# Expert weights as whole matrices, a dense gather of two units, and the last modulation vector beside the router

## The chip, the cores and the metric

The kernel runs on one core of a Trainium2 chip. The core has TensorE (PE in the rows; the loading of its stationary operand has a row of its own, PEld), VectorE (DVE), ScalarE (ACT), GpSimd (POOL) and SyncE (SP), which here only issues transfers. Every load from HBM goes through one queue, in the order in which SP issues it, and 16 DMA engines move the bytes. The metric is the device time of one execution in microseconds; lower is better. The profile is of one execution on the chip; its span runs from the first instruction to the last.

## The reference, cut to what matters

Two blocks follow each other on x (256 tokens by 1024). The first has attention, a gated delta rule and a mixture of experts; its output is normalised and goes into the second, a transformer block whose shifts, scales and gates (`mod`, six vectors of 1024) come from a conditioning vector, and whose attention also looks at 256 context tokens. Cut:

```python
# first block, at its end
h = rmsnorm(x, ffn_norm)
g_sel = argmax(h @ w_group)                   # one of 4 groups
within = top2(softmax((h @ w_router)[g_sel])) # two of its 8 experts, weights normalised
for e in all 32 experts:
    y += ((silu(h @ w_gate[e]) * (h @ w_up[e])) * combine[:, e]) @ w_down[e]   # 1024x256, 1024x256, 256x1024
x = rmsnorm(x + y, final_norm)
# second block
mod   = split(silu(c) @ w_mod + b_mod, 6)     # w_mod is 1024x6144
mod_c = the same with c_ctx
hc = rmsnorm(ctx) * (1 + scale_c) + shift_c   # keys and values of the context: hc @ w_in
x = x + g1 * attention(rmsnorm(x) * (1 + scale) + shift, hc)
x = x + g2 * swiglu(rmsnorm(x) * (1 + scale2) + shift2)
```

## The kernel before

The program has stages: "a" (first attention and delta rule, with its weights split into a high and a low part so that three float32r products stand for one float32 product), "c" (router and experts) and "d" (second block). A scheduler orders the instructions of each engine when the program is built; where `PE.start()` and `PE.stop()` enclose code, the order on TensorE is that in which the code is written.

All large weights come in blocks of 1 MiB (128 partitions by 2048 float32), `load_block`, line 157. Each takes a buffer: one of a ring of nine, or, in the expert stage, one of the further pools named in `SLOTS` ("r" ring, "x" three, "y" seven, "z" two, which is 21 with the ring). A block is issued when its buffer is free, and SP issues in a fixed order, so one block that waits holds up all behind it.

The experts run in eight units of four. Each unit has room for 32 tokens of each of its experts. Per unit:

- `gather(u)` (line 1051) picks the tokens with a one-hot matrix S: 16 matmuls in float32 of x against S, in two halves, each evicted with the gain `gF` into `xg`.
- gate and up (`pgu`): for each of 8 slices k and each of the 4 experts j one matmul in a quarter of the array's columns. `wexp` (line 1027) cuts the four gate matrices by k: block q holds the slices 2q and 2q+1 of all four experts, so its rows in HBM are four pieces of 2 KB a partition.
- the hidden values are turned (`pth`), then `pyd`, the down products in two halves nh of 512 columns; a block of `w_down` is one (nh, k2) of four experts.
- each half is split into yh and yl and added into four PSUM banks `acc` through a one-hot matrix ST.

At unit 4 (`IFU`) the order changes: only ring and "x" buffers stay, plus two of a new pool "w". The context is loaded, normalised through diagonal matrices (`ctx_norm`), and four of its five projections (`ctx_heads`, with the columns of w_in in `KVU`) run between the products of units 5 and 6, where the scheduler puts them. `kv_a` and `qk_heads` each hold a head norm (ACT square, DVE sum, GpSimd power, DVE product) and then transposes on TensorE. A branch, `overflow()`, stands ahead of unit 4 for experts with over 32 tokens.

The modulation vectors: `mod_steps` yields once per block of `w_mod`, 24 in all, 8 matmuls each. `more_mod` takes such steps as filler inside stage "a", by the numbers in `MODR` (in the triangular solves) and `MODS` (behind the projections). At the router a loop takes whatever is left.

In the profile, a float32 matmul shows as two records on TensorE, and a float32r matmul as one.

Of the kernel before, what the change touches and what calls it, by code (L numbers as in the profile page):

```python
# [9 lines left out]
F32 = mybir.dt.float32  # L10
# [7 lines left out]
P = 128  # L18
# [87 lines left out]
def tile_kernel(ctx: ExitStack, tc: tile.TileContext, I, out, dbg=None):  # L106
# [9 lines left out]
    def open_stage(name, psum, base=False):  # L116
# [9 lines left out]
        S_["junk"] = {"a": ("zg", 2), "c": ("jk", 1), "d": ("prb2", NPR)}[name]  # L126
# [30 lines left out]
    def load_block(src, name, extra=None):  # L157

        if extra:
            t = extra[0].tile([P, 2048], F32, tag="rx", name=name, bufs=extra[1])  # L160
# [219 lines left out]
    def mod_steps():  # L380


        for n in range(6):
            p = psm([P, 256], "pmod", "mo")
# [11 lines left out]
            part = tmp_([P, 8, 32], "part", "part")  # L396
            DVE.transpose(part, p.rearrange("p (c k) -> p k c", k=8))
            DVE.tensor_tensor(mod[:, n], part[:, :, 0::16], bc(bmc[:, n], 2), op=ALU.add)
            if n in (1, 4):
                DVE.scalar_tensor_tensor(mod[:, n], mod[:, n], 1.0, bc((gN1, gN2)[n // 4], 2), op0=ALU.add, op1=ALU.mult)  # L400
            yield
# [373 lines left out]
    def out_steps():  # L775
        for kb in (2, 3, 0, 1):
            hi, lo = w_blk[kb]
            for kk in range(2):
                k = 2 * kb + kk
                for tt in range(2):  # L780
                    ts = slice(tt * P, (tt + 1) * P)
                    for nh in range(2):
                        ns = slice(nh * 512, nh * 512 + 512)
                        mm3(po2[2 * tt + nh], mixh[:, k, ts], mixl[:, k, ts], hi[:, kk, ns], lo[:, kk, ns], k == 4, k == 3)
                        yield
# [85 lines left out]
    rx3p = rx2.enter_context(tc.tile_pool(name="rx3", bufs=1, side="right", reuse_waits="tile"))  # L871
# [18 lines left out]
    for tt in range(2):  # L890
        jk = tmp_([P, D], "jk", "jk", bufs=2, dt=BF16)
        if tt == 0:
            i = ACT.activation(jk, x[:, 0], AF.Square, accum_out=ssq[:, 0:1])
# [7 lines left out]
    S_["mod"] = None  # L901
    for _ in mods:
        if S_["mod"]:
            after(S_["mod"], pl_ins)
# [55 lines left out]
    PE.matmul(prk[:, 1], lhsT=trisb, rhs=sel[:, 1], start=False, stop=True)  # L960
    rrp = at([P, 2, 32], "rrp", "rrp")
# [9 lines left out]
    def one_hots(g):  # L971
        S[g] = at([P, 2, 8, 32], "S", "S")
        for ts in (slice(0, 1), slice(1, 2)) if g == 0 else (slice(0, 2),):
            DVE.tensor_tensor(S[g][:, ts], io[:, None, None, :].to_broadcast([P, ts.stop - ts.start, 8, 32]),
# [3 lines left out]
    one_hots(0)  # L978
    pov = psm([1, 1], "pov")
# [29 lines left out]
    DVE.tensor_tensor(ovc, ovm, comb, op=ALU.mult)  # L1009
# [4 lines left out]
    DVE.tensor_copy(combr[:, :, :, 4:6], r1[:, :, None, None].to_broadcast([P, 2, 8, 2]))  # L1014

# [4 lines left out]
    pools = {"r": None, "x": (S_["base"], RX), "y": (rx2p, RX2), "z": (rx3p, RX3)}  # L1020
# [6 lines left out]
    def wexp(w, u, part, name):  # L1027
# [25 lines left out]
    def gather(u):  # L1053

        if u % 2 == 0 and u:
            one_hots(u // 2)
        xg = c2.tile([P, 8, P], F32, tag="xg", name=f"xg{u}", bufs=2)
        for kp in range(2):
            p = pt_([P, 4, P], "y", "pgat")
            for kk in range(4):  # L1060
                for tt in range(2):
                    PE.matmul(p[:, kk], lhsT=x[:, tt, 4 * kp + kk::8], rhs=S[u // 2][:, tt, u % 2 * P:u % 2 * P + P],
# [782 lines left out]
```

## Time and profile before

| | us |
|---|---|
| three timed runs, median (lowest to highest) | 851.44 (848.9 to 851.9) |
| the profiled execution, its own time | 851.4 |
| span of that execution | 849.6 |

| engine | busy us | share of the span | instructions |
|---|---|---|---|
| TensorE (matmul) | 784.6 | 92% | 6412 |
| TensorE (weight load) | 647.7 | 76% | 6412 |
| VectorE | 424.1 | 50% | 937 |
| ScalarE | 296.1 | 35% | 526 |
| GpSimd | 107.4 | 13% | 93 |

200.18 MB are moved, 236 GB/s over the span. A share is a mean over stages with different limits, so it says little by itself: the transfers are near their limit for half of the time and almost idle for the other half. What a part of the change is worth is read from its stage: which wait ends last there. A buffer that comes free late shows as a wait of the transfer queue for an engine, and only later as a wait of an engine for data. The granted clock of TensorE has two levels, 2.4 GHz (1.00 in the windows) and 1.2 GHz (0.50); a stretch between is a mixture.

### The profile page before, as it was taken

Reading aid. Unit: us, or ns where it says so; the run is one execution under the profiler, and the core shown is the slowest. Engines: PE = TensorE matmul, PEld = TensorE weight load, DVE = VectorE, ACT = ScalarE, POOL = GpSimd, SP = SyncE. Lnnn points to the kernel's source line nnn. Section 1 sums busy time; section 2 is a strip of 40 time slices with the busy share of each in tenths; the row PEclk is TensorE's granted clock in tenths of the full one; section 3 lists DMA queues with packets and bytes.
Section 4 is the critical chain, followed back from the end, with each engine's and each line's share of the span. In section 5 each row is a group of like instructions: output and inputs, shape, how many; then the busy total and the mean of one; then the engine's idle time right before and its main releaser. Section 6 shows DMA issues by size and latency. Waiting matters only on the chain.

```text
span 849.6 us, 15290 instructions
## 1 busy us (share of the span) xinstructions
PE 784.6 (92%) x6412; PEld 647.7 (76%) x6412; DVE 424.1 (50%) x937; ACT 296.1 (35%) x526; POOL 107.4 (13%) x93
## 2 busy tenths in 40 slices
PE   7999999999789989896998899799996999999997
PEld 6887887967656646673865799688875999999996
DVE  4766553565422111223132769887656555455545
ACT  5432233453110000101011765287723444434431
POOL 5001000142000000000000376400021200000000
PEclk9999999999889998987999999899999999999999
DMA  7999778488799999999599506111431756555201
GB/s 212 350 385 380 278 284 305 171 308 302 279 388 386 386 386 387 378 386 370 198 390 377 169 5 161 59 51 50 150 105 47 257 188 197 179 174 193 100 2 49
DMA packets 123415, 200.18 MB, mean 236 GB/s; under 512 B 15480, under 2 KB 62000, under 8 KB 123344
## 3 DMA queue, kind: packets, MB, share of 16 engines
q1 hardware_dynamic: 123152, 199.08, 67.3%
q8 instruction: 51, 0.84, 0.4%
q0 software_dynamic: 192, 0.11, 0.1%
q14 instruction: 20, 0.16, 0.1%
HBM read 198.23 MB, written 1.05 MB: 235 GB/s over the span
## 4 chain that ended last, share of the span: by engine, by line
PE 46%; DVE 7%; POOL 3%; ACT 2%; issue 2%; POOLq 0%; DVEq 0%; ACTq 0%
PE pfu L99 7%; PE pfg L99 7%; PE pf L99 7%; PE sc L99 3%; PE pgat L99 3%; PE pgu L99 2%; PE po L99 2%; PE ptp L102 2%; PE pyd L99 2%; PE ckbp L99 2%; PE pqa L99 1%; PE pqb L99 1%; POOL latl L192 1%; PE acc L99 1%; PE pt L99 1%
## 5 line engine op out<-in xcount | busy, mean ns | idle before, releaser
L99 PEld LDWEIGHTS pgat<-S,x 128*128 128x128 f32 x256 | 62.4, 335 | 2.8 <-DVE xg L1066 1.1
L99 PE MATMUL pgat<-S,x 128*128 128x128 f32 x256 | 63.0, 405 | 0.6 <-PEq L1215 0.5
L99 PE MATMUL pfu<-hif,fuh 128*128 128x256 f32 x176 | 50.3, 286 | 1.6 <-ACT fuh L185 1.6
L99 PE MATMUL pfu<-hif,ful 128*128 128x256 f32 x176 | 50.5, 287 | 0.9 <-POOL ful L192 0.8
L99 PE MATMUL pfu<-lof,fuh 128*128 128x256 f32 x176 | 50.2, 285 | 0.0
L99 PE MATMUL pfg<-hif,fgl 128*128 128x256 f32 x160 | 45.5, 284 | 0.0
L99 PE MATMUL pfg<-lof,fgh 128*128 128x256 f32 x160 | 45.5, 284 | 0.0
L99 PE MATMUL pfg<-hif,fgh 128*128 128x256 f32 x160 | 45.5, 284 | 0.0
L1066 DVE TENSOR_TENSOR xg<-pgat,cols__83 128x512 f32<-128x512 f32 x15 | 10.4, 692 | 63.8 <-PE pgat L99 63.8
L192 DVE TENSOR_TENSOR fdl<-fd,fdh 128x512 fp32r<-128x512 f32 x44 | 27.5, 688 | 28.8 <-ACT fdh L185 28.8
L99 PE MATMUL pyd<-ed,hid 128*32 128x512 f32 x256 | 34.1, 665 | 3.8 <-ACT hid L1341 3.8
L1335 ACT ACTIVATE sg<-pgu,r1s 128x256 f32<-128x256 f32 x8 | 3.8, 474 | 96.6 <-PE pgu L99 73.9
L99 PEld LDWEIGHTS pfu<-hif,fuh 128*128 128x128 f32 x176 | 34.3, 195 | 1.8 <-ACT fuh L185 1.8
L99 PEld LDWEIGHTS pfu<-hif,ful 128*128 128x128 f32 x176 | 34.3, 195 | 1.3 <-POOL ful L192 1.3
L99 PE MATMUL pf<-fdl,fh 128*128 128x512 f32 x88 | 35.1, 399 | 0.0
L185 ACT ACTIVATE fuh<-fu 128x1024 fp32r<-128x1024 f32 x22 | 22.1, 1053 | 37.0 <-issue 28.6
L185 ACT ACTIVATE fdh<-fd 128x1024 fp32r<-128x1024 f32 x22 | 22.1, 1053 | 36.8 <-issue 35.8
L99 PE MATMUL pf<-fdh,fh 128*128 128x512 f32 x88 | 34.7, 394 | 0.0
L99 PEld LDWEIGHTS pfu<-lof,fuh 128*128 128x128 f32 x176 | 34.2, 194 | 0.0
L99 PE MATMUL pf<-fdh,fl 128*128 128x512 f32 x88 | 34.0, 392 | 0.0
L192 DVE TENSOR_TENSOR fgl<-fg,fgh 128x512 fp32r<-128x512 f32 x40 | 27.7, 755 | 9.3 <-ACT fgh L185 9.3
L99 PEld LDWEIGHTS pfg<-hif,fgh 128*128 128x128 f32 x160 | 30.9, 193 | 0.4
(704 smaller groups left out, 2156.6 us busy)
## 6 DMA issues: line engine op xcount, KB each, us to landing
eg<-in_w_gate_dram SPq DMA_DIRECT2D x32, 1024.0 KB, 14.0
eu<-in_w_up_dram SPq DMA_DIRECT2D x32, 1024.0 KB, 13.9
ed<-in_w_down_dram SPq DMA_DIRECT2D x32, 1024.0 KB, 13.4
wmod<-in_w_mod_dram SPq DMA_DIRECT2D x24, 1024.0 KB, 10.3
fg<-in_w_gate_dram SPq DMA_DIRECT2D x11, 1024.0 KB, 5.6
fu<-in_w_up_dram SPq DMA_DIRECT2D x11, 1024.0 KB, 5.7
fd<-in_w_down_dram SPq DMA_DIRECT2D x11, 1024.0 KB, 5.1
kv<-in_w_in_dram SPq DMA_DIRECT2D x5, 1024.0 KB, 13.5
```

The lines of the kernel that those rows point to most:

```text
L99: return self._keep(self.engine.matmul(*args, **kwargs))
L102: return self._keep(self.engine.transpose(*args, **kwargs))
L185: S_["hi"] = ACT.activation(hf[:, s], vf[:, s], AF.Copy)
L192: i = (POOL if c in pool else DVE).tensor_tensor(lf[:, s], vf[:, s], hf[:, s], op=ALU.subtract)
L1066: DVE.tensor_tensor(xg[:, ks], p, bc(gF[:, ks], P), op=ALU.mult)
L1335: ACT.activation(sg, pgu[:, 0], AF.Silu, scale=r1s[:, u:u + 1])
```

## The change

1. An expert's gate, up or down matrix is one block: 128 partitions by one piece of 8 KB. Block j now belongs to expert j, so each pass needs all four blocks from its start, and frees them at its end.
2. x is split into xhi and xlo (float32r, laid out by slices k). `gather(g)` serves two units: 32 float32r matmuls of 256 columns, four evictions. Unit 2 adds xhi and xlo into `acc` by an identity, so the adds of x behind unit 7 go, and x's own memory becomes a buffer ("p").
3. The buffers are ring nine, x three, y seven, p one: 20. "z" is gone, and "w" has one in place of two.
4. From unit 4 to the end of unit 7 TensorE's order is as written. Projections of the context stand between gate and up, and, with the turning of the hidden values between their halves, ahead of down. Both down halves stand ahead of the splits and of acc. The context's rows are scaled ahead of plain transposes. Columns 1792 are used in unit 5, given up and loaded again for the second block.
5. Twenty blocks of w_mod are left in stage "a"; the last vector's four come behind the blocks of w_out, three are multiplied behind the logits and the fourth behind the ranks. Its PSUM bank is that of acc2.
6. The last block of the first output projection runs by halves of the tokens.

```diff
 def wexp(w, u, part, name):
...
-        src = w[u // 2, 4 * (u % 2):4 * (u % 2) + 4]
-        if name == "ed":
-            src = src.rearrange("e (p k) c -> p e k c", k=2)[:, :, part % 2, part // 2 * 512:part // 2 * 512 + 512]
-        else:
-            src = src.rearrange("e (p k) c -> p e (k c)", k=8)[:, :, part * 512:part * 512 + 512]
+        src = w[u // 2, 4 * (u % 2) + part].rearrange("(p k) c -> p k c", p=P)
...
+    xhi, xlo = (at([P, 2, 8, P], nm, nm, dt=F32R) for nm in ("xhi", "xlo"))
+    identr = at([P, P], "identr", "identr", dt=F32R)
+    for tt in range(2):
+        xk = x[:, tt].rearrange("t (p k) -> t k p", k=8)
+        after(ACT.activation(xhi[:, tt], xk, AF.Copy), jk_ins)
+
+    PE.start()
+    for i in range(3):
+        next(mods)
...
+    pmod5 = next(mods)
...
     one_hots(0)
+    xk = x.rearrange("t a (p k) -> t a k p", k=8)
+    for i in range(4):
+        ks = slice(2 * i, 2 * i + 2)
+        S_["xlo"] = DVE.tensor_tensor(xlo[:, :, ks], xk[:, :, ks], xhi[:, :, ks], op=ALU.subtract)
+        after(S_["xlo"], S_["S"])
...
-    pools = {"r": None, "x": (S_["base"], RX), "y": (rx2p, RX2), "z": (rx3p, RX3)}
+    pools = {"r": None, "x": (S_["base"], RX), "y": (rx2p, RX2), "p": (pers, 1, "x")}
...
+    def gather(g, tags=("y", "y")):
+
+        if g:
+            one_hots(g)
+        xg = [c2.tile([P, 4, 256], F32, tag="xg", name=f"xg{g}", bufs=2) for _ in range(2)]
+        for kp in range(4):
+            p = pt_([P, 2, 256], tags[kp % 2], "pgat")
+            for kk in range(2):
+                parts = [(tt, xp) for xp in (xhi, xlo) for tt in range(2)]
+                for n, (tt, xp) in enumerate(parts):
+                    PE.matmul(p[:, kk], lhsT=xp[:, tt, 2 * kp + kk], rhs=S[g][:, tt], start=n == 0, stop=n == 3)
...
+    CTX = {4: (None, None), 5: ((1792, lambda b=None: ctx_v(0, b)), (512, ctx_ka)),
+           6: ((1280, lambda b=None: ctx_kb(0, b)), (1536, lambda b=None: ctx_kb(1, b))), 7: (None, None)}
...
             if half == 0:
                 gate_ins = last
+                if u == 4:
+                    hcT = ctx_norm()
+                elif u > 4 and CTX[u][0]:
+                    CTX[u][0][1]()
...
+        if u >= IFU and CTX[u][1]:
+            CTX[u][1][1](turn_hid)
+        else:
+            turn_hid()
...
-MODR = [2, 2, 2, 2, 2, 2]
-MODS = [0, 1, 2, 0, 1, 0, 1, 0, 2, 2, 2, 2, 2, 1, 0, 0, 0, 0]
+MODR = [2, 2, 2, 1, 1, 1]
+MODS = [0, 1, 1, 0, 1, 0, 1, 0, 1, 2, 1, 2, 1, 0, 0, 0, 0, 0]
...
-SLOTS = "r" * 4 + "ry" * 4 + "yyyr" + "xz" * 2 + "x"
+SLOTS = "r" * 4 + "ry" * 4 + "yyyr" + "xxxp"
...
-KVU = ((512, 1280), (1536, 1792), (), (2048,))
```

What this moves on the engines, at three places. First the transfer queue of SP behind the last block of w_out (`wo`), up to the first expert blocks (`eg`, `eu`, `ed` are gate, up and down). Before:

```order
L164 DMA wo_2328<-in_w_out_dram 128x2x1024
L164 DMA eg<-in_w_gate_dram 128x4x512 x4
L164 DMA eu<-in_w_up_dram 128x4x512 x3
L164 DMA ed<-in_w_down_dram 128x4x512 x2
L164 DMA eg<-in_w_gate_dram 128x4x512
L164 DMA eu<-in_w_up_dram 128x4x512
L164 DMA eg<-in_w_gate_dram 128x4x512 x2
```

After, the same place:

```order
L164 DMA wo_2284<-in_w_out_dram 128x2x1024
L164 DMA wmod<-in_w_mod_dram 128x2x1024 x4
L164 DMA eg<-in_w_gate_dram 128x2048
L164 DMA eu<-in_w_up_dram 128x2048 x2
L164 DMA ed<-in_w_down_dram 128x2048 x2
L164 DMA eg<-in_w_gate_dram 128x2048 x6
L164 DMA eu<-in_w_up_dram 128x2048 x5
```

Four blocks of w_mod now stand ahead of the experts, and an expert block has one run of 2048 where it had four of 512.

Second, TensorE from the logits (`pl`) over the ranks (`prk`) to the first gate products. Before:

```order
L99 MATMUL pl<-wr,hT 128x36 x16
L99 LDWEIGHTS trisb
L99 MATMUL prk<-sel,trisb 128x32
...
L99 MATMUL pov<-ones_96,ovn 1x1
L99 MATMUL pgat<-S,x 128x128 x16
L99 MATMUL pgu<-eg,xg_2635 32x256 x32
```

After:

```order
L99 MATMUL pl<-wr,hT 128x36 x16
L99 MATMUL pmod<-wmod,sil 32x256 x24
L99 LDWEIGHTS trisb
L99 MATMUL prk<-sel,trisb 128x32
...
L99 MATMUL pmod<-wmod,sil 32x256 x8
L99 MATMUL pov<-ones_96,ovn 1x1
L99 MATMUL pgat<-S,xhi 128x256 x2
L99 MATMUL pgat<-S,xlo 128x256 x2
```

The products of the last modulation vector stand on both sides of the ranks, and the gather takes two columns of S's halves at once, from xhi and then from xlo.

Third, TensorE in the seventh unit, from its gate products to its down products (`ckbp` is a projection of the context, `pqk` the transposes behind its head norm). Before:

```order
L99 MATMUL pgu<-eg,xg_3885 32x256 x32
L99 MATMUL pgu<-eu,xg_3885 32x256 x15
L102 MATMUL pqk<-cst,qn__3935 128x128 x4
L99 MATMUL cvbp<-kv_3958,hcT 128x256 x16
L99 MATMUL pgu<-eu,xg_3885 32x256 x17
L99 LDWEIGHTS esel
L99 MATMUL pst<-rrT,esel 128x256
L102 MATMUL pth<-cst,sg 128x128 x2
L99 MATMUL pyd<-ed,hid 32x512 x16
```

After:

```order
L99 MATMUL ckbp<-kv_3953,hcT 128x256 x16
L102 MATMUL pqk<-cst,qn__4023 128x128 x4
L99 MATMUL pgu<-eu,xg_3893 32x256 x16
L99 MATMUL pgu<-eu,xg_3894 32x256 x16
L99 LDWEIGHTS esel
L99 MATMUL pst<-rrT,esel 128x256
L99 MATMUL ckbp<-kv_3963,hcT 128x256 x8
L102 MATMUL pth<-cst,sg 128x128 x2
L99 MATMUL ckbp<-kv_3963,hcT 128x256 x8
L102 MATMUL pqk<-cst,qn__4105 128x128 x4
L99 MATMUL pyd<-ed,hid 32x512 x16
```

Both transposes behind a head norm now stand directly behind the projection that feeds the norm, and ahead of up and of down.

## Rows read from the trace of the kernel before

**Rows 1.** The page, 40 slices of 21.24 us: what the transfers moved

```profile
GB/s 212 350 385 380 278 284 305 171 308 302 279 388 386 386 386 387 378 386 370 198 390 377 169 5 161 59 51 50 150 105 47 257 188 197 179 174 193 100 2 49
```

**Rows 2.** Windows: length, busy us of five engines (instructions), granted clock, DMA share, GB/s

```profile
6.00:10.00 4.00, 2.58 (x21) 2.21 (x20) 1.98 (x8) 1.59 (x3) 2.14 (x4) 1.00 1.07 355
...
50.00:100.00 50.00, 49.17 (x523) 41.17 (x522) 30.50 (x87) 15.85 (x33) 5.94 (x5) 1.00 0.95 349
...
82.00:88.00 6.00, 5.89 (x54) 5.86 (x51) 2.58 (x8) 1.02 (x2) 2.03 (x4) 1.00 1.02 410
...
228.00:232.00 4.00, 4.00 (x74) 2.42 (x77) 0.69 (x1) 0.00 (x0) 0.00 (x0) 1.00 0.33 71
...
240.00:246.00 6.00, 5.53 (x33) 1.23 (x32) 0.69 (x1) 0.98 (x2) 0.00 (x0) 0.59 1.04 385
...
270.00:290.00 20.00, 18.41 (x187) 13.72 (x189) 3.32 (x9) 0.86 (x2) 0.00 (x0) 1.00 1.05 387
...
414.00:424.00 10.00, 10.00 (x88) 8.20 (x90) 1.55 (x3) 0.60 (x1) 1.30 (x1) 1.00 0.09 19
```

**Rows 3.** Waits of TensorE, 50 to 200 us: total, times, longest us

```profile
PE pkq L99 <- DVE kn L594: 0.7, 1, 0.7
...
PE po L99 <- ACT mixh L758: 0.2, 1, 0.2
```

**Rows 4.** Groups of TensorE, 228 to 470 us: busy us, mean ns, idle before

```profile
L99 PE MATMUL pgat<-S,x 128*128 128x128 f32 x226 | 55.8, 402 | 0.5 <-PEq L1215 0.5
```

**Rows 5.** Timeline of SP's issues: start us, length us, transfer, count

```profile
2.62 1.53 SPq L164 DMA_DIRECT2D w<-in_w_in_dram  x2
...
70.94 25.07 SPq L164 DMA_DIRECT2D wmod<-in_w_mod_dram  x6
...
402.78 20.58 SPq L164 DMA_DIRECT2D ed<-in_w_down_dram  x4
...
441.23 12.92 SPq L164 DMA_DIRECT2D ed<-in_w_down_dram  x4
```

**Rows 6.** Waits of the transfer queue, 400 to 430 us: total, times, longest us

```profile
SPq L164 <- PE pgu L99: 18.8, 5, 17.2
```

**Rows 7.** Timeline of TensorE: start us, length us, output, count, idle before and releaser

```profile
142.30 1.93 PE L99 MATMUL pmod<-wmod,sil 128*32 128x256 f32 x30
...
228.27 3.66 PE L99 MATMUL pgu<-eg,xg 128*32 128x256 f32 x64
...
240.65 5.72 PE L99 MATMUL pyd<-ed,hid 128*32 128x512 f32 x32 [0.47 <-ACT hid L1341]
...
288.62 3.64 PE L99 MATMUL pyd<-ed,hid 128*32 128x512 f32 x32 [0.47 <-ACT hid L1341]
...
293.44 3.85 PE L99 MATMUL pgat<-S,x 128*128 128x128 f32 x16
...
383.03 4.05 PE L99 MATMUL ckbp<-kv,hcT 128*128 128x256 f32 x18
...
391.23 0.69 PE L102 MATMUL pqk<-cst,qn__3725 128*128 128x128 f32 x4 [3.15 <-DVE qn__3725 L1104]
394.97 0.39 PE L99 MATMUL pst<-rrT,esel 32*128 32x256 bf16 x1 [3.05 <-DVE kLb L1166]
...
465.02 1.92 PE L99 MATMUL pyd<-ed,hid 128*32 128x512 f32 x16
468.13 0.73 PE L99 MATMUL acc<-yh,ST 128*128 128x512 f32 x2 [1.19 <-ACT yh L1352]
```

**Rows 8.** Timeline of VectorE, columns as in rows 7

```profile
219.95 0.76 DVE L974 TENSOR_TENSOR S<-cst,rrp 128x256 f32<-128x256 f32 x2
...
469.39 1.28 DVE L1359 TENSOR_TENSOR x<-x,acc 128x512 f32<-128x512 f32 x2 [0.59 <-PE acc L99]
```

**Rows 9.** The chain that ended last: start us, length us, what

```profile
735.97 5.75 PE pfg L99 x48
```

**Rows 10.** The page's groups: busy us, mean ns, idle before

```profile
L1335 ACT ACTIVATE sg<-pgu,r1s 128x256 f32<-128x256 f32 x8 | 3.8, 474 | 96.6 <-PE pgu L99 73.9
```

More of the change, by code (lines that the diff above doesn't have):

```diff
@@ L159, in load_block @@
         if extra:
-            t = extra[0].tile([P, 2048], F32, tag="rx", name=name, bufs=extra[1])
+            t = extra[0].tile([P, 2048], F32, tag=extra[2] if len(extra) > 2 else "rx", name=name, bufs=extra[1])
         else:
@@ L395, in mod_steps, with mod_end @@
                     yield
[L396 to L401, printed above, removed]
+            if n < 5:
+                mod_end(n, p)
+                yield
+        yield p
+    def mod_end(n, p):
+        part = tmp_([P, 8, 32], "part", "part")
+        S_["part"] = DVE.transpose(part, p.rearrange("p (c k) -> p k c", k=8))
+        DVE.tensor_tensor(mod[:, n], part[:, :, 0::16], bc(bmc[:, n], 2), op=ALU.add)
+        if n in (1, 4):
+            DVE.scalar_tensor_tensor(mod[:, n], mod[:, n], 1.0, bc((gN1, gN2)[n // 4], 2), op0=ALU.add, op1=ALU.mult)
     MODA = MODS[:14]
@@ L1199, in proj_ctx, with ctx_v, ctx_ka, ctx_kb @@
                 S_["cx"].append(m)
-        return p
-    def ctx_heads():
-        kv_a(proj_ctx(512, "cka"), 1, "tr")
-        yield
-        for half in range(2):
-            qk_heads(proj_ctx(1280 + 256 * half, "ckb"), half, 3, "tr", s=1)
-            yield
-        for half in range(2):
-            S_["vb"] = (ACT.copy if half else DVE.tensor_copy)(vb[1][:, :, half * 256:half * 256 + 256], proj_ctx(1792 + 256 * half, "cvb"))
-            yield
+            if tt == 0 and between:
+                between()
+        return p
+    def ctx_v(half, between=None):
+        p = proj_ctx(1792 + 256 * half, "cvb", between)
+        S_["vb"] = (ACT.copy if half else DVE.tensor_copy)(vb[1][:, :, half * 256:half * 256 + 256], p)
+    def ctx_ka(between=None):
+        kv_a(proj_ctx(512, "cka", between), 1, "tr")
+    def ctx_kb(half, between=None):
+        qk_heads(proj_ctx(1280 + 256 * half, "ckb", between), half, 3, "tr", s=1)
     def overflow():
@@ L1219, in overflow @@
                 for tt in range(2):
-                    PE.matmul(p[:, tt * P:(tt + 1) * P], lhsT=x[:, tt, k::8], rhs=ident, start=True, stop=True)
+                    for xp in (xhi, xlo):
+                        PE.matmul(p[:, tt * P:(tt + 1) * P], lhsT=xp[:, tt, k], rhs=identr, start=xp is xhi, stop=xp is xlo)
                 DVE.tensor_scalar(hT[:, k], p, gF[:, k:k + 1], None, op0=ALU.mult)
@@ L1272, in tile_kernel @@
             c2 = S_["tmp"]
-        if u not in xgs:
-            xgs[u] = gather(u)
+        if u // 2 not in xgs:
+            xgs[u // 2] = gather(u // 2, ("y", "y" if u < IFU else "cx"))
         if u and u % 2 == 0:
@@ L1295, in tile_kernel @@
                 DVE.tensor_copy(gcol[:, i:i + 1], pgc[:, 0:1])
-            ring_slot()
-            cx = load_block(I["ctx_2"][0].rearrange("(a p) d -> p a d", p=P), "cx")
+            PE.start()
         if u == 5:
-            hcT = ctx_norm()
             queue.append("r")
-        if u >= 5:
-            for c0 in KVU[u - 5]:
-                ring_slot()
+        first.setdefault(u, [])
+        for i, (w, nm) in enumerate(((wg_, "eg"), (wu_, "eu"), (wd_, "ed"))):
+            if len(first[u]) == i:
+                first[u].append([wexp(w, u, q, nm) for q in range(4)])
+            if u >= IFU and i < 2 and CTX[u][i]:
+                c0 = CTX[u][i][0]
+                if c0 != 1792:
+                    ring_slot()
                 kvw[c0] = load_block(cols(w_in2, c0), f"kv{c0}")
-                next(ctxh)
-        if u not in first:
-            loads(u)
         if u == 7:
@@ L1328, in tile_kernel @@
             acc = [psm([P, 512], "acc0"), psm([P, 512], "acc1", "mo")] + [accp_.tile([P, 512], F32, tag=f"acc{i}", name=f"acc{i}") for i in (2, 3)]
+        if u == 2:
+            for tt in range(2):
+                for nh in range(2):
+                    for xp in (xhi, xlo):
+                        PE.matmul(acc[2 * tt + nh], lhsT=identr, rhs=xp[:, tt, :, 64 * nh:64 * nh + 64].rearrange("t k p -> t p k"),
+                                  start=False, stop=False)
         p = pt_([P, 256], "tr", "pst")
```

125 lines of the change are left out of this document (60 added, 65 removed).

## The prediction

> **What bounds the kernel now.** I read four views, in this order. The 40 slices of the page [rows 1] first: from about 230 us to 460 us the transfers run at 386 to 390 GB/s with one hole, and after 480 us they never matter again. So only the first 480 us can react to how the experts are loaded; the last 370 us are the second block, which the change leaves alone apart from how x is stored. The windows [rows 2] give the stream's speed and its holes: 387 GB/s in 270 to 290 us, 19 GB/s in 414 to 424 us (10 us lost) while TensorE is busy all 10 us, and 71 GB/s in 228 to 232 us, where all 21 buffers are full and unit 0 has not yet freed one. What the transfer queue waited for in 400 to 430 us is TensorE: 17.2 us in one wait [rows 6], and the four down loads of unit 6 take 20.58 us to issue [rows 5]. So the stage has two limits by turns: the stream from 232 to about 345 us, and TensorE in the units that also carry the context's projections. TensorE's largest group there is the gather, 55.8 us for 226 records [rows 4]. Ahead of 205 us TensorE is the limit: 49.17 of 50 us busy [rows 2], and from 50 to 200 us it waits 3.4 us in six waits of 0.7 to 0.2 us, none of them for a transfer [rows 3].
>
> **The change part by part.** All sums stand against the profiled execution: span 849.6 us, 851.4 us with the 1.8 us around it, which is the median of the runs shown (851.44 us).
>
> *Whole matrices.* The same 96 MiB are loaded, but one row of a partition is now 8 KB in one piece and not four pieces of 2 KB. What size of piece does to the speed is in the windows [rows 2]: pieces of 1 KB (w_in, 6 to 10 us) move at 355 GB/s, of 2 KB (experts, 270 to 290 us) at 387, of 4 KB (w_mod, 82 to 88 us) at 410; what was on its way then is in the queue's rows [rows 5]. One block of 1 MiB then takes 2.95, 2.71 and 2.56 us. 8 KB is not in the trace. Each halving of the number of pieces saved less, 0.24 and then 0.15 us, so the next saves some 0.08: 2.48 us. The other end is 2.56 us, if a piece of 8 KB does no better than 4 KB, and 2.71 if nothing is gained. I take 2.52, midway of the first two, since those lie on the curve. At the point where the stream starts again after the router 76 of 96 blocks are still to come (20 buffers full), so 76 x (2.71 - 2.52) = 14.4 us less, between 0 and 17.5.
>
> *The gather.* Before, each unit had 16 matmuls of float32 with 128 columns in two halves of about 3.85 us, as at 293.44 us [rows 7], 7.7 us a unit, 62 us in all. Now two units share 32 float32r matmuls of 256 columns. Matmuls of that shape run one per 0.12 us in the feed-forward part (48 in 5.75 us [rows 9]), so 3.8 us for two units, 15 us in all: 46 us of TensorE less. The stream is slower than this work, so by itself it gives nothing; it gives back the hole at 414 to 424 us, 10 us. In units 0 to 3 TensorE then needs 3.7 + 3.6 + 3.6 + 2.9 + 1.9 us and some 2 us of small products, about 18, against 12 x 2.52 = 30 us of stream. In unit 6 it needs gather 3.8, gate 3.7, projection 7.2, the wait of a head norm, up 3.6, projection 7.2, another wait, down 3.6, acc 2.9. The wait is from the end of the projection at 387.08 to the transposes at 391.23 us [rows 7], 4.15 us, and the fixed order puts nothing of TensorE into it. Sum 40.3 us, against 36.1 us of stream (12 expert blocks, two of w_in). Unit 5 with one such wait needs 33 against 36. So TensorE ends unit 6 some 4 us later than its data, frees its down buffers that late, and unit 7's stream waits some 2 us for them: +2, between 0 and +6. Net of the hole: -8.
>
> *First unit.* DVE must now write the four xlo parts (512 columns, 0.64 us each by the adds of that shape [rows 8]) after S, which is ready at 220.7 us [rows 8]; ACT's xhi lies beside the logits. Gather, its eviction on ACT (eight of 0.47 us [rows 10]) and the gate overlap by parts, so the gate ends near 227.5 us and not 231.9 [rows 7]: 4 us earlier. But there are 20 buffers and not 21, and four of them hold w_mod until its products behind the logits free them at about 217 us; the queue then has eight blocks to bring from 209.7 us, to about 230 us. At 231.5 us, where the stream began again before with 21 blocks in, 20.6 are in: 0.4 blocks, +1.0 us, between -1 and +3. The hole at 228 us is gone, and the 21st buffer that hid it too, so it gives nothing more.
>
> *The last modulation vector.* Its four blocks cost TensorE 30 records in 1.93 us [rows 7], 64 records in 4.1 us, in a stretch where TensorE is the limit. They go to where it waits for DVE's choice of experts. Three of the four blocks were filler inside the triangular solves, where less filler can turn into a wait, so I take 2.5 of the 4.1 us: -2.5, between 0 and -4.1. Everything behind moves with it. The DVE part (one transpose, one add) comes behind the routing weights, where DVE has nothing else that the gather needs; without that cover it would stand ahead of the first eviction, at well under the 0.64 us of a full tile [rows 8].
>
> *The end of the stage.* Before, the last down load is issued by 454.15 us [rows 5], and its products come in two halves with the acc products between, the second at 465.02 us, the last acc product done near 469.6 us [rows 7]. In whole matrices all 32 products need the block of the fourth expert: 3.6 us after the last landing and not 1.9. At the lower clock level (0.59 granted in 240 to 246 us [rows 2]) the same 32 took 5.72 us [rows 7], and TensorE will have waited for data. So +2, between +0.5 and +4. The adds into x (two of 0.64 us [rows 8]) are gone from the path since x is summed in PSUM; eight products of x stand in unit 2 instead, where there is slack: -0.7, between 0 and -1.3.
>
> *At nothing:* context rows scaled ahead and not by a diagonal (off the path while TensorE has slack; it shortens unit 4 by some 6 us of slack), kv 1792 loaded a second time behind the stage, where the stream is idle [rows 1], the order of the last out-projection block (x adds begin 1.4 us earlier, TensorE runs straight on there).
>
> Sum: -14.4 - 10 + 2 + 1.0 - 2.5 + 2 - 0.7 = -22.6. Span 827.0, with 1.8 around it **828.8 us**. With all ends at their best 818, at their worst 854; all at one end is unlikely, so 818 to 837 is the forecast's own range.
>
> **Rivals.**
>
> *Pieces of 8 KB are no faster.* Then the first part does not do what it says: 387 GB/s stay, 14.4 us are lost, 843.2 us. Against it: 355, 387, 410 GB/s rise with the piece [rows 2]. For it: nothing here shows a piece over 4 KB, and the load of one matrix may be limited elsewhere. The Trainium skill, DMA: Bandwidth & Descriptors, section "Where 436 GB/s comes from", says that loads from HBM are bound at about 358 GB/s per core. By that the stream could not gain and this rival would be the result; the rows at 387 and 410 GB/s already stand above it, so I give it little weight.
>
> *The fixed order waits.* In units 5 and 6 TensorE stands at three head norms in a row. If each costs more than 4.15 us (at 394.97 us the trace has another wait of 3 us for the same PSUM bank's copies) and the projection behind it starts at the lower clock level, its 7.2 us growing to up to 14, TensorE ends unit 6 some 14 us behind its data and not 4. Unit 7's buffers come 10 us later: 838.8 us. For it: the stall that made the hole at 414 us began behind the first of these norms. Against it: in the new order the transposes of the hidden values stand between the halves of the projection, so that DVE and ACT work beside it.
>
> *TensorE goes slow (the slower side).* With 18 us of work in 30 us it now waits for each set of four matrices, and none of a set can start until the fourth is there. In units 4 to 7 it has 4 x 14 + 7.7 + 4 x 7.2 + 2 = 94.5 us of work in 135 us of stream. At half clock each of these costs another; 40 us are covered by waiting, and after that each comes out at the end. The 22.6 us are eaten when 63 of the 94.5 run at the lower level; with all of them 883 us. For it: 0.59 in 240 to 246 us, 5.72 us and not 3.64 for the same products [rows 2, 7]. Against it: in 270 to 290 us, with waits for the hidden values in it, the clock is 1.00, and a TensorE that falls behind no longer waits. The Trainium skill, TensorE: Matmul & The Clock Gate, section "Loop structure matters more than you think", warns of just this loop, a wait for a transfer between groups of matmuls; the 240 us row agrees, and by it this rival would be likelier than I make it.
>
> **How the numbers follow.** Forecast 828.8 us with chance 0.64; fixed order 838.8 with 0.15; no faster pieces 843.2 with 0.12; TensorE slow, 855 to 883, with 0.05; something not seen 0.04, half of it slower. The range 816 to 841 holds the forecast, the fixed order's case and the lower edge of the third. About 0.5% (4.3 us) is what a measurement of this kernel can tell from no change. Faster by more: 0.89; within: 0.04; slower: 0.07.
>
> **What would show each step.** Windows of the expert stage at 410 to 423 GB/s, not 387, show the first term; a window without a hole around units 5 to 7, and a transfer queue that waits little for TensorE, show the second. The gather's group should read 128 records, and 15 us, not 62. The first out-projection and the router should come 2 to 3 us earlier, the first gate near 225 us, the last acc product near 447 us, and from there to the end some 380 us as before. A granted clock under 0.8 over most of units 4 to 7, or down products that stand behind the head norms with the queue idle, would make it wrong; so would a first unit whose down blocks land after 240 us.

## The result: 11.7 us less, where 22.6 were forecast

| | before | after | ratio (95% interval) |
|---|---|---|---|
| timed runs, median (lowest to highest) | 850.97 us (848.9 to 851.9) | 839.32 us (836.76 to 841.26) | 0.9865 (0.9826 to 0.9904) |
| the same two kernels, measured again | 852.27 us (849.43 to 853.69) | 837.18 us (832.93 to 839.01) | 0.984 (0.9818 to 0.9861) |

The change is faster, by 11.7 us, and by 15.1 in the second measurement (differences of the medians). The forecast was 828.8 us, 22.6 less, with a range of 816 to 841 that holds the result near its upper end. The profiled execution of after took 841.26 us (span 839.5). It is read here against the one of before (851.4 us, span 849.6).

What the transfers moved, in the page of after (40 slices of 20.99 us):

```profile
GB/s 219 343 389 346 213 251 331 102 313 294 396 369 419 420 418 417 387 409 407 414 308 297 135 20 178 30 52 51 152 146 33 272 171 182 201 175 178 100 2 50
```

The 386 of [rows 1] have become 420, but one larger dip is left: 308 in the slice from 420 us. Windows of after, columns as in [rows 2]:

```profile
219.00:222.00 3.00, 2.65 (x23) 1.86 (x14) 3.00 (x7) 0.20 (x1) 0.00 (x0) 0.65 1.00 407
222.00:225.00 3.00, 3.00 (x19) 2.17 (x18) 2.93 (x13) 1.54 (x4) 0.00 (x0) 0.50 1.01 418
...
231.00:234.00 3.00, 3.00 (x64) 1.80 (x60) 0.00 (x0) 0.00 (x0) 0.00 (x0) 1.00 0.49 128
...
270.00:290.00 20.00, 18.36 (x211) 8.77 (x203) 3.85 (x7) 2.05 (x4) 0.00 (x0) 1.00 1.01 420
420.00:430.00 10.00, 5.85 (x30) 2.44 (x32) 3.96 (x8) 1.96 (x3) 1.64 (x1) 0.74 0.87 360
430.00:440.00 10.00, 9.63 (x120) 4.62 (x112) 2.16 (x4) 1.20 (x2) 0.00 (x0) 0.92 0.66 247
```

A block of 1 MiB takes 2.50 us at 420 GB/s, where it took 2.71. The hole that lay at 414 to 424 us is in 420 to 440 us now, about half as large: (420 - 360) and (420 - 247) GB/s over ten us each are 5.5 us of the stream. The clock column shows 0.50 and 0.65 in the gather of the first unit, and a hole at 231 to 234 us behind it. What the transfer queue waited for in 400 to 440 us:

```profile
SPq L164 <- PE pyd L99: 17.2, 1, 17.2
SPq L164 <- PE pst L99: 9.9, 1, 9.9
```

It still stands behind TensorE for 17.2 us in one wait, as in [rows 6], now for the down products. Here they are, with the passes ahead of them (timeline of TensorE, columns as in [rows 7]):

```profile
229.18 2.37 PE L99 MATMUL pgu<-eg,xg 128*32 128x256 f32 x40
...
380.73 5.12 PE L99 MATMUL pyd<-ed,hid 128*32 128x512 f32 x32
...
408.00 1.12 PE L102 MATMUL pqk<-cst,qn__4023 128*128 128x128 f32 x4 [4.06 <-DVE qn__4023 L1122]
409.04 4.63 PE L99 MATMUL pgu<-eu,xg 128*32 128x256 f32 x64
...
425.37 1.09 PE L102 MATMUL pqk<-cst,qn__4105 128*128 128x128 f32 x4 [4.15 <-DVE qn__4105 L1122]
426.38 6.18 PE L99 MATMUL pyd<-ed,hid 128*32 128x512 f32 x32
...
448.79 5.21 PE L99 MATMUL pyd<-ed,hid 128*32 128x512 f32 x26 [1.57 <-DMA ed<-in_w_down_dram]
```

The two head norms of unit 6 cost 4.06 and 4.15 us, as priced. But up takes 4.63 us behind the first, and down 6.18 us behind the second, where passes of the same size take 3.66 and 3.64 us at the higher level [rows 7]; the 5.12 us are the down products of unit 5, behind a norm too. And TensorE's groups from 205 to 470 us (columns as in [rows 4]):

```profile
L99 PE MATMUL pyd<-ed,hid 128*32 128x512 f32 x256 | 43.1, 727 | 4.6 <-ACT hid L1389 2.4 <-DMA ed<-in_w_down_dram 2.2
...
L99 PE MATMUL pgat<-S,xhi 128*128 128x256 f32 x64 | 15.2, 320 | 0.9 <-DVEq L1237 0.9
L99 PE MATMUL pgat<-S,xlo 128*128 128x256 f32 x64 | 14.2, 306 | 0.3 <-DVE xlo L995 0.3
```

The same group before:

```profile
L99 PE MATMUL pyd<-ed,hid 128*32 128x512 f32 x256 | 34.1, 665 | 3.8 <-ACT hid L1341 3.8
```

The down products take 43.1 us in all, 727 ns each, where as many products of the same size took 34.1 us (665 ns). The last acc product ends at 457.0 us, where it ended at 469.6: the expert stage gave 12.6 us of the 22.6, and the rest of the span, the second block, is 2.5 us longer in this execution.

### The profile page after: what moved, and what is told of

Same layout as the page of the kernel before. It is cut to its first block, busy times and chain, and to the rows that moved or that the text cites. A ratio compares the mean times of both kernels' runs of the same rounds, so it can differ in the third digit from the quotient of the medians.

```text
span 839.5 us, 15017 instructions
## 1 busy us (share of the span) xinstructions
PE 763.3 (91%) x6276; PEld 608.4 (72%) x6276; DVE 424.3 (51%) x933; ACT 302.9 (36%) x533; POOL 108.0 (13%) x94
## 4 chain that ended last, share of the span: by engine, by line
PE 43%; DVE 6%; DMA 3%; POOL 2%; ACT 2%; issue 2%; SPq 0%; DVEq 0%; POOLq 0%; ACTq 0%
PE pfu L99 8%; PE pfg L99 7%; PE pf L99 7%; PE sc L99 3%; PE po L99 2%; PE ptp L102 2%; PE pyd L99 2%; PE pgu L99 2%; DMA kv<-in_w_in_dram 2%; PE ckbp L99 2%; PE pqa L99 1%; PE pqb L99 1%; DMA ed<-in_w_down_dram 1%; PE cvbp L99 1%; POOL rq L218 1%
## 5 line engine op out<-in xcount | busy, mean ns | idle before, releaser
L99 PE MATMUL pyd<-ed,hid 128*32 128x512 f32 x256 | 43.1, 727 | 4.6 <-ACT hid L1389 2.4
L99 PE MATMUL pgu<-eu,xg 128*32 128x256 f32 x512 | 36.2, 411 | 3.8 <-DMA eu<-in_w_up_dram 3.7
L99 PE MATMUL pgu<-eg,xg 128*32 128x256 f32 x512 | 34.0, 385 | 1.1 <-DVE sg L1375 1.1
L1400 DVE TENSOR_TENSOR yl<-pyd,yh 128x512 fp32r<-128x512 f32 x16 | 11.1, 691 | 44.5 <-ACT yh L1399 35.8
L99 PEld LDWEIGHTS pyd<-ed,hid 128*32 128x32 f32 x256 | 9.9, 129 | 31.5 <-issue 22.7
## 6 DMA issues: line engine op xcount, KB each, us to landing
ed<-in_w_down_dram SPq DMA_DIRECT2D x32, 1024.0 KB, 15.4
```

The costliest lines, as they stand in the source:

```text
L99: return self._keep(self.engine.matmul(*args, **kwargs))
L1400: DVE.tensor_tensor(yl, py, yh, op=ALU.subtract)
```

## Experiments

The expected texts below weigh theories by letter. Theory W: TensorE ends unit 6 late, by the waits at the head norms and by the lower clock behind them, and the stream stops for its buffers. Theory B, its rival: the buffers themselves, one fewer, and given back four at once. The two were told apart first by moving the work of unit 6.

**The transposes one pass later (defer).** The transposes behind each head norm are put in a list and issued behind the next pass.

```diff
-        pt = pt_([P, 2, 256], tag, "pqk")
+        def turn_qk():
+            pt = pt_([P, 2, 256], tag, "pqk")
...
+        late.append(turn_qk)
...
+        if late:
+            late.pop(0)()
         sg = c2.tile([P, 256], F32, tag="sg", name="sg", bufs=3)
...
-        pys = [pt_([P, 512], t, "pyd") for t in ("y", "y" if u < IFU else "cx")]
+        pys = [pt_([P, 512], t, "pyd") for t in ("y", "y" if u < IFU else ("gu" if late else "cx"))]
+        if late:
+            late.pop(0)()
         for nh, py in enumerate(pys):
             yh = c2.tile(
```

> Only the order is changed: the transposes behind the three head norms of the context's projections stand one pass later (unit 5 and the second of unit 6 behind the down products, the first of unit 6 behind the up products), and the second down half uses the bank of gate and up. Theory W (the hole of the stream at 425 to 437 us is TensorE ending unit 6 late, by the head norms' waits of 3.56, 4.06 and 4.15 us and the lower clock behind them): TensorE ends unit 6 over 10 us earlier than at 435 us, the queue's longest wait for the down products falls from 17.2 to under 6 us, no 10 us of 420 to 440 us stays under 390 GB/s, time 832 to 834 us. Theory B (the hole is the buffers: one fewer, and a pass of whole matrices gives back all four at its end): the hole stays where TensorE does not matter, time 838 to 841 us.

Measured 832.23 us, ratio 0.9762 (0.9731 to 0.9793). Its TensorE in unit 6, and its windows:

```profile
415.85 3.64 PE L99 MATMUL pyd<-ed,hid 128*32 128x512 f32 x32
420.07 0.63 PE L102 MATMUL pqk<-cst,qn__4105 128*128 128x128 f32 x4 [0.58 <-DVE qn__4105 L1122]
```

```profile
420.00:430.00 10.00, 7.58 (x80) 3.98 (x80) 3.88 (x7) 1.66 (x3) 0.00 (x0) 1.00 1.01 420
430.00:440.00 10.00, 6.79 (x61) 2.79 (x61) 0.00 (x0) 0.00 (x0) 0.00 (x0) 0.66 1.02 419
```

Down runs at 3.64 us and is done at 419.5 and not 432.6 us, and the hole is gone. The buffers are the same, so B alone does not make the hole; whether a further buffer would have closed it too was not tried.

**The scheduler's order (free).** `PE.start()` at unit 4 and `PE.stop()` behind unit 7 are left out.

> The changed kernel without the fixed order from unit 4 on: the scheduler places TensorE's work of units 4 to 7, and it puts the transposes behind the head norms behind other products. Theory W: the waits for the head norms fall to under 2 us each, unit 6 ends 5 to 10 us earlier, 833 to 837 us. Theory B: 838 to 842 us.

Measured 830.41 us, ratio 0.9755 (0.973 to 0.9781), less than the band named: the lowest median of this study, though too near defer and the next kernel to be told from them, and faster than the kernels before and after. The stream stays whole in the same place:

```profile
420.00:430.00 10.00, 6.25 (x74) 2.77 (x78) 0.53 (x2) 0.00 (x0) 0.00 (x0) 0.88 1.01 421
```

**The clock apart from the wait (warm_heads).** Both of these take away the waits and the slow passes together. This one keeps the waits and fills them with products whose results nothing uses:

```diff
+        if s == 1:
+            warm(7)
         pt = pt_([P, 2, 256], tag, "pka")
...
+    def warm(n):
+        pw = pt_([P, 256], "y", "pwm")
+        for _ in range(n):
+            PE.matmul(pw, lhsT=hcT[:, 0, 0:P], rhs=hcT[:, 1], start=True, stop=True)
...
         head_norm(p, 4, n_, "rq")
+        if s == 1:
+            warm(8)
```

> The changed kernel with idle products (float32, 128x256, into a bank that is overwritten) in TensorE's three waits for head norms: 7 in unit 5, 8 in each of the two of unit 6, some 3.2 and 3.6 us; nothing of the result uses them. The waits stay as long as they were. Theory C (half of the lateness is the lower clock behind the waits): up of unit 6 and down of units 5 and 6 fall from 4.63, 5.12 and 6.18 to 3.64 us, unit 6 ends some 5 us earlier, 834 to 836 us. Theory L (the waits' length alone counts, or the clock does not rise): 838 to 841 us.

Measured 831.27 us, ratio 0.9761 (0.973 to 0.9792), some 3 us less than the band named. Its TensorE in unit 6 and at the end of unit 7, its windows, and the queue's longest wait in 400 to 440 us:

```profile
402.05 3.62 PE L99 MATMUL pwm<-hcT 128*128 128x256 f32 x16
406.27 0.66 PE L102 MATMUL pqk<-cst,qn__4031 128*128 128x128 f32 x4 [0.61 <-DVE qn__4031 L1122]
406.86 3.66 PE L99 MATMUL pgu<-eu,xg 128*32 128x256 f32 x64
...
422.77 3.64 PE L99 MATMUL pyd<-ed,hid 128*32 128x512 f32 x32
...
443.26 3.62 PE L99 MATMUL pyd<-ed,hid 128*32 128x512 f32 x26 [1.51 <-DMA ed<-in_w_down_dram]
```

```profile
420.00:430.00 10.00, 8.25 (x55) 3.71 (x54) 5.26 (x9) 2.56 (x4) 1.34 (x1) 1.00 1.01 418
430.00:440.00 10.00, 8.56 (x136) 4.58 (x135) 0.87 (x2) 0.86 (x2) 0.00 (x0) 1.00 1.01 419
```

```profile
SPq L164 <- PE pyd L99: 13.3, 1, 13.3
```

Idle products of 3.62 us and 0.61 us of waiting make up the old 4.2 us, but up and down run at 3.66 and 3.64 us. Unit 6's last down product ends at 426.4 and not 432.6 us, and no hole follows, though the queue still waits 13.3 us; in both profiles of after it waits 15.9 us or more there, and a hole follows. What was issued ahead of the wait seems to cover the shorter one: a down block lands 15.4 us after its issue (the median in the page of after), so that is about how long it lasts, an estimate.

The first unit is that of after's profile (the first gate ends at 231.6 us), so the difference lies behind it. The last acc product ends at 449.9 and not 457.0 us, 7.1 us earlier. Of these, 1.6 us are the last down pass (3.62 and not 5.21 us), whose wait was not filled, and 1.1 were won ahead of the first filled wait, where a projection of unit 5 took 7.14 and not 8.82 us. So C holds, the waits being as long as before and the passes behind them no longer slow, and it is worth some 4.5 us by these two profiles, an estimate (7.1 - 1.6 - 1.1). The medians differ by 8.1 us (839.32) and by 5.9 (837.18), but not all of that is C: the second block, which the edit leaves alone, is 3.3 us shorter in this profile than in that of after.

**A projection moved to unit 7 (ctx7).**

```diff
-           6: ((1280, lambda b=None: ctx_kb(0, b)), (1536, lambda b=None: ctx_kb(1, b))), 7: (None, None)}
+           6: ((1280, lambda b=None: ctx_kb(0, b)), None), 7: ((1536, lambda b=None: ctx_kb(1, b)), None)}
```

> The second key projection of the context (columns 1536) goes from unit 6 to unit 7, between gate and up, with its load; nothing else. Theory W: unit 6 loses 7.2 us of projection, one wait of 4.15 us and the slow passes behind it, ends near 421 us and not 435, the hole closes, and the projection in unit 7 lies in the wait for the last down blocks: 832 to 835 us. Theory B: hole unchanged, 838 to 842 us, since the end of unit 7 only gets longer.

Measured 845.02 us, ratio 0.9909 (0.9873 to 0.9945): slower than after, though the stream has 400 and 413 GB/s in 420 to 440 us, and above the bands of both theories. Its unit 7:

```profile
421.63 3.66 PE L99 MATMUL pgu<-eg,xg 128*32 128x256 f32 x64
433.21 9.46 PE L99 MATMUL ckbp<-kv,hcT 128*128 128x256 f32 x32 [7.92 <-DMA kv<-in_w_in_dram]
446.73 1.12 PE L102 MATMUL pqk<-cst,qn__4199 128*128 128x128 f32 x4 [4.05 <-DVE qn__4199 L1122]
447.77 5.51 PE L99 MATMUL pgu<-eu,xg 128*32 128x256 f32 x64
```

The hole closed, as W said, but my expectation that the projection would lie in a wait was wrong. Its block stands behind the four of up in the queue and comes at 433 us, it starts at the lower level (9.46 us), and its head norm then stands between all the data, which is there, and up. A hole in the middle of the stream was traded for a chain at its end.

**What whole matrices are worth: the old cutting in the changed kernel (cut2k), in the kernel free (cut2k_free), and whole matrices in the kernel before (before_whole).** For cut2k and cut2k_free these lines are as in the kernel before; before_whole has the reverse.

```diff
-        src = w[u // 2, 4 * (u % 2) + part].rearrange("(p k) c -> p k c", p=P)
+        src = w[u // 2, 4 * (u % 2):4 * (u % 2) + 4]
...
-                                     rhs=ww[j][:, k], start=k == 0, stop=k == 7)
+                                     rhs=ww[k // 2][:, j, k % 2 * 256:k % 2 * 256 + 256], start=k == 0, stop=k == 7)
...
-                              rhs=dw[j][:, k2, nh * 512:nh * 512 + 512], start=k2 == 0, stop=k2 == 1)
+                              rhs=dw[2 * nh + k2][:, j], start=k2 == 0, stop=k2 == 1)
```

> The changed kernel with the old cutting of the blocks (a block is a slice of four experts, four pieces of 2 KB a partition), all else kept. Theory W: the rate falls from 419 to 387 GB/s, 2.50 to 2.71 us a block, some 77 blocks, +16 us; of it some 7 us come back, since a slower stream does not wait for unit 6, and 2 to 3 us since blocks of a pass come free one after the other: 845 to 849 us. Theory B (whole matrices give back by late buffers what they gain in speed): 838 to 842 us.

> The kernel before with whole matrices alone (the block is one expert's matrix, and the products take it so); float32 gather, buffers, scheduler's order and modulation vectors stay. Theory W: the rate rises to 419 GB/s, 2.50 us a block, but from unit 4 on TensorE is the limit (gather 7.7 us a unit and the projections), so only what is gained up to there counts, some 45 blocks x 0.21 us = 9 us, and the hole of the stream grows past 10 us: 841 to 845 us. Theory S (the rate alone decides): 16 us less, 834 to 837 us. Theory B (late return of buffers eats it): 848 to 852 us.

> The kernel free with the old cutting in pieces of 2 KB: what whole matrices are worth where TensorE does not hold up the stream. Theory W (stream-bound): 77 blocks x (2.71 - 2.50) = 16 us over free, 2 to 3 back since blocks come free one after the other: 843 to 846 us, about as long as with the fixed order (846.8), since a slower stream hides the head norms' waits. Theory P (TensorE holds up this kernel too, so that the rate is worth as little as it was in the kernel before): 833 to 837 us.

| median us | pieces of 2 KB | whole matrices | gain |
|---|---|---|---|
| kernel before | 851.26 | 853.03 | none: ratio 1.0026 (0.9999 to 1.0053) |
| changed, fixed order | 846.77 | 839.32, 837.18 | 7.5 to 9.6 |
| changed, scheduler's order | 846.38 | 830.41 | 16.0 |

One edit, three prices. The rate is the same wherever whole matrices are loaded. In before_whole, two windows and the queue's longest wait of 340 to 440 us:

```profile
270.00:290.00 20.00, 18.39 (x193) 12.08 (x193) 2.95 (x5) 1.45 (x3) 0.00 (x0) 1.00 1.01 421
...
410.00:420.00 10.00, 9.96 (x99) 7.51 (x99) 2.24 (x4) 1.00 (x2) 1.64 (x1) 1.00 0.05 8
```

```profile
SPq L164 <- PE pgu L99: 47.1, 4, 18.8
```

The blocks come at 421 GB/s, and then the queue waits 47.1 us for TensorE's gate and up, with 8 GB/s in the ten us from 410, while TensorE is busy for 9.96 of them with the float32 gather, a projection and unit 6's gate. The time is the one I gave for B, 1 us beyond its band; the trace shows W's reason, since the stream runs at 416 to 421 GB/s from 250 to 330 us, where blocks are given back four at once as well. What my W had wrong is that the gain up to unit 4 would stay: it was given back in units 5 to 7, and the last acc product ends at 470.2 us (469.6 before). With the dense gather, and in the order that keeps the stream whole through unit 6 (free), the whole 16 us appear, as 77 blocks x 0.21 us say.

The old cutting takes the same time under either order (846.8 and 846.4), but not because a slower stream hides the waits, as I had expected. Windows of cut2k, then of cut2k_free:

```profile
440.00:450.00 10.00, 7.46 (x42) 2.78 (x43) 5.26 (x9) 2.56 (x4) 1.29 (x1) 0.83 0.48 152
```

```profile
440.00:450.00 10.00, 8.71 (x97) 3.60 (x89) 3.94 (x7) 0.83 (x2) 0.00 (x0) 1.00 1.05 389
```

The fixed order has its hole behind unit 6 at 386 GB/s too, and the last acc product ends 3.4 us later there (467.2 and 463.8 us). The second block is 4.0 us shorter in that profile, so the totals agree. Why whole matrices bring only 7.5 to 9.6 us under the fixed order is therefore left open.

**The last modulation vector back in the first stage (modback, and free_modback with the scheduler's order).** The tables `MODR` and `MODS` are those of before, `mod_end` runs for all six vectors in `mod_steps`, and the three places behind the router are left out.

```diff
-MODR = [2, 2, 2, 1, 1, 1]
+MODR = [2, 2, 2, 2, 2, 2]
...
-    pmod5 = next(mods)
...
-    mod_end(5, pmod5)
```

> The changed kernel with the last modulation vector back in the first stage (24 blocks of w_mod there, none ahead of the experts, the old two tables of numbers); all else kept. By the prediction's terms: 2.5 us more ahead of the router, 1 us less behind it, 839 to 842 us. Theory M (the four blocks of w_mod hold buffers and time of the stream where the experts' loads should run ahead): the stream has over 1.5 blocks more at 235 us, 834 to 837 us.

> The changed kernel as it is, once more, beside the next one on the same chip, since 839.3 and the 835.6 us with the last modulation vector back are near each other's spread. Theory T (moving the vector is worth nothing or a little): 836 to 839 us, within 3 us of 835.6. Theory M (moving it costs): 839 to 841 us, its interval apart from that of the kernel with the vector back.

> Both edits that were faster: the scheduler's order from unit 4 on, and the last modulation vector back in the first stage. Theory T: the vector's place does not matter where the stream has no hole, 829 to 833 us. Theory M: the four blocks no longer stand ahead of the experts, 3 to 4 us less than 830.4: 826 to 828 us.

modback 835.55 us, ratio 0.9805 (0.9776 to 0.9834); after once more 837.18, 0.984 (0.9818 to 0.9861); free_modback 832.48, 0.9781 (0.976 to 0.9803), against 830.41 for free. The first pair says that the move costs 1.6 us (3.8 against the first measurement of after), the second that it saves 2.1, and the intervals of each pair overlap. So the place of the vector is worth nothing that these runs can tell; M is not borne out, though modback's time lies in the band that I gave for it, nor is the net 1.5 us of the prediction. In modback's trace the stream after the first unit is no further on, against M: its queue stands in 231 to 235 us too, though no block of w_mod is ahead of the experts there.

```profile
231.00:235.00 4.00, 4.00 (x80) 2.25 (x72) 0.00 (x0) 0.00 (x0) 0.00 (x0) 1.00 0.58 178
```

The second profile of after (832.93 us, span 831.2) told more than its median. It is the same program, 8.3 us shorter. Windows, then TensorE:

```profile
222.00:225.00 3.00, 3.00 (x36) 1.98 (x29) 2.59 (x14) 1.52 (x4) 0.00 (x0) 1.00 1.03 426
...
231.00:234.00 3.00, 2.04 (x19) 1.19 (x11) 1.29 (x6) 1.23 (x1) 0.00 (x0) 1.00 1.00 404
...
420.00:430.00 10.00, 8.00 (x44) 3.05 (x44) 5.26 (x9) 2.56 (x4) 0.75 (x1) 0.83 0.62 229
```

```profile
225.59 2.37 PE L99 MATMUL pgu<-eg,xg 128*32 128x256 f32 x40
...
377.01 3.64 PE L99 MATMUL pyd<-ed,hid 128*32 128x512 f32 x32
...
403.83 6.10 PE L99 MATMUL pgu<-eu,xg 128*32 128x256 f32 x64
...
422.18 5.34 PE L99 MATMUL pyd<-ed,hid 128*32 128x512 f32 x32
...
443.64 3.62 PE L99 MATMUL pyd<-ed,hid 128*32 128x512 f32 x26 [1.39 <-DMA ed<-in_w_down_dram]
```

In this execution the clock stayed at 1.00 through the first gather, the first gate ends at 228.0 and not 231.5 us, and the queue does not stand behind it (404 GB/s, not 128). The last down products run at 3.62 and not 5.21 us. Behind unit 5's norm, a wait of 3.55 us, down runs at full speed (3.64 us), so not every such wait is followed by a slow pass; behind the two norms of unit 6 up and down are slow again (6.10 and 5.34 us). The hole behind unit 6 is there in both.

**Idle products at two other waits (free_warm).** Four products of the size of warm_heads behind the logits, eight ahead of the second block's first scores, on the kernel free.

> The kernel free with idle products in two other waits: four (1.8 us) behind the logits, ahead of the ranks, and eight ahead of the second block's first scores, where the profile of the changed kernel shows the lower clock in 530 to 548 us. Theory C (the clock falls in the wait and its time is lost to the result): from the ranks to the end of the first gate 10.7 us, the scores at 0.74 us and not 1.20 for four, 2 to 4 us less than free: 826 to 829 us. Theory N (the clock falls for reasons that these products do not touch): 829.5 to 833 us.

Measured 832.77 us, ratio 0.979 (0.9765 to 0.9814): no gain over 830.41. The first scores:

```profile
523.70 0.72 PE L99 MATMUL sc<-k,qa 128*128 128x256 f32 x4
524.30 0.72 PE L99 MATMUL sc<-k,qa 128*128 128x256 f32 x4
529.00 1.23 PE L99 MATMUL sc<-k,qa 128*128 128x256 f32 x4 [3.91 <-ACT prb L1623]
530.12 1.20 PE L99 MATMUL sc<-k,qa 128*128 128x256 f32 x4
```

The clock was up for the first scores (0.72 us for four, not the 1.20 to 1.22 of free), as C said. But TensorE then came to the next wait, 3.91 us for ACT's exponentials, and ran at 1.20 behind that. From the first scores to the first feed-forward product it is 109.0 us, in free 107.4. So Theory N's time came out, not its reason: there is another wait right behind. The four products behind the logits had nothing to show: from the ranks to the end of the first gate it is 11.0 us with them, and was 10.7 in free's profile without them.

**Where the profiles differ.** The same four points of each profile, in us, read from TensorE's timeline:

| | ranks begin | first gate ends | last acc product ends | from there to the end |
|---|---|---|---|---|
| before | 219.2 | 231.9 | 469.6 | 380.0 |
| after | 218.4 | 231.5 | 457.0 | 382.5 |
| after_again | 217.3 | 228.0 | 450.3 | 380.9 |
| warm_heads | 218.4 | 231.6 | 449.9 | 379.2 |
| defer | 221.5 | 232.2 | 451.0 | 379.6 |
| free | 217.0 | 227.7 | 445.0 | 383.7 |
| cut2k | 217.3 | 228.0 | 467.2 | 378.6 |
| cut2k_free | 218.5 | 231.6 | 463.8 | 382.6 |

The last column moves by 5 us, and by 3.9 between after and cut2k, whose code is the same there. A difference of a few us between two single profiles is therefore no effect of an edit unless its place is shown.

## Why the prediction was right and wrong

*Whole matrices: right, a little better.* 2.50 us a block for the 2.52 taken (420 GB/s). The rival that pieces of 8 KB are no faster falls. By the rule from the Trainium skill, DMA: Bandwidth & Descriptors, "Where 436 GB/s comes from" (about 358 GB/s per core from HBM), the rate could not have risen; 420 here decides against it, for this core alone.

*The gather: right in work, and half of the hole stayed.* 32 products take 4.1 us, from 388.4 to 392.5 us (3.8 forecast). The sign that I named, 15 us for the group, was badly chosen: the two groups above add up records that overlap, 29.4 us for the 128. The step that failed is the "+2" for unit 6. I gave TensorE 40.3 us there, with the two waits at 4.15 us and every pass at its fast price. The waits came to that; but up and down behind them took 4.63 and 6.18 us, and unit 5's down 5.12 us, so TensorE was some 5 us later still (unit 6 ends at 432.6 us, and at 426.4 in warm_heads), and the queue's wait outlasted what was issued ahead of it. The term was not +2 but, by the medians of defer, free and warm_heads, +5 to +9 (832.2, 830.4, 831.3 against 839.3 and 837.2). The row for it was in my own text, 5.72 us for the down products at 240.65 us [rows 7]; I used it only for the end of the stage and for the rival where TensorE is slow all along.

*The rival of the fixed order* gave 838.8 us with a chance of 0.15, and the result is its number (839.3 and 837.2), at its place: the norms of unit 6 and the queue behind them. Its own account was off: the norms did not take more than 4.15 us, and the projections behind them ran at full speed (7.17 us, and 3.72 with 3.62); the passes behind the waits were slow. The rival where TensorE is slow came true for a small part: by the group of down products, 43.1 - 34.1 = 9.0 us over all units. The Trainium skill, TensorE: Matmul & The Clock Gate, "Loop structure matters more than you think", warns of a long wait for a transfer between matmuls. The rows at 4.63 and 6.18 us agree for the pass behind a wait, though these waits are for VectorE and some 4 us long, and the loop as a whole was not slow. The 240 us row that the prediction puts beside this warning does not show its case: the waits just ahead of it in the trace are 0.4 to 1.5 us long and for VectorE and ScalarE, not for a transfer.

*First unit: right in direction, half of the size.* The gate ended at 228.0 us in the second profile (227.5 forecast), and at 231.5 in the first. That 228.0 is so near is in part luck, since the ranks begin 1.9 us earlier in that profile than before. From the ranks to the end of the gate it is 12.7 us before, 10.7 where the clock stayed up and 13.2 where it did not: 2.0 us less or 0.5 more, for the 4 forecast. An xlo part takes 1.02 us (4.09 for four), not the 0.64 taken, but only 0.35 us of that is waited for in the first profile and 0.55 in the second. In the first profile the gate came 3.5 us later than in the second, and the stream waited; the +1.0 for the buffers cannot be read apart from that.

*The last modulation vector: not shown.* In six profiles whose instructions up to there are the same, the ranks begin between 217.0 and 221.5 us (219.2 before), so a term of 2.5 us cannot be read from one profile, and the timed pairs disagree in sign.

*The end of the stage: right in kind.* The last 26 down products took 5.21 us in one profile and 3.62 in the other, against 1.92 for the last half before; the +2 was between.

*The second block: a spread, and no term of the change.* From the last acc product to the end it is 380.0 us before, 382.5 and 380.9 after, and 378.6 to 383.7 in the others of the table. The first scores ran at a clock of 0.51 in 16 us of after, at 0.75 in those of before:

```profile
532.00:548.00 16.00, 13.71 (x65) 12.28 (x65) 11.96 (x32) 9.62 (x26) 1.40 (x1) 0.51 0.00 1
```

```profile
544.00:560.00 16.00, 14.21 (x92) 12.69 (x91) 13.78 (x39) 11.89 (x31) 1.41 (x2) 0.75 0.01 2
```

(The first window is of after, the second of before.) The code of the scores is the same. Why one execution gets the higher level sooner than another is left open; no run here tells.

Together: the forecast was 8.4 to 10.5 us too low, and the range held the result because it was drawn to hold the fixed order's 838.8 as well. One of the signs named for being wrong did show, down products behind a head norm while the queue stands. The kernels without slow passes behind the three norms measure 830.4 to 832.2 us, near 828.8, but that is in part luck: the vector's 2.5 us cannot be told from nothing, the first gate came 2 us earlier at best and not 4, and free still has slow passes in unit 7 (up 6.24, down 5.36 us).

## What to carry to other kernels

Price a pass that stands behind a wait of TensorE at the lower clock level, not only the wait: here three waits of some 4 us cost nothing that these runs can tell once they were filled, and the slow passes behind them cost some 4.5 us by the profiles, and 6 to 8 by the medians, where chance takes part. Fill such a wait with products that nothing uses, or put the work that waits one pass later; but look first at which wait is next, since a faster engine may only arrive at it sooner. And the worth of a faster stream depends on what takes the blocks: the same edit gave 0, 8 to 10 and 16 us in three surroundings.

## What the runs showed of the chip

In loads of 1 MiB, pieces of 8 KB a partition move at 418 to 421 GB/s on one core, against 410 for 4 KB and 386 for 2 KB. A single wait of 4.05 to 4.15 us was followed by a pass of 4.63 to 6.18 us that takes 3.64 to 3.66 at full clock. Two executions of one program differed by 8.3 us in span (839.5 and 831.2); 2.5 us of it lie in the first gather and gate and 1.6 in the last down pass, where one of them ran at the lower clock, 1.1 in when the ranks begin and 1.6 in the second block; the rest was not followed. From the first rank product to the end of the first gate it was 10.7 us where the clock stayed up and 13.2 where it did not.
